# A head's maximum written to the query tile by ScalarE, without a transfer

## The chip, the core and the metric

The kernel runs on one NeuronCore of a Trainium2 chip. The core has five engines that run beside each other and wait for one another by semaphores: TensorE (PE: matmuls, with PEld for its weight loads), VectorE (DVE), ScalarE (ACT), GpSimd (POOL) and SyncE (SP, which issues most DMAs). Sixteen DMA engines move data between HBM and the on-chip memory SBUF; matmul results land in PSUM. The metric is device time in microseconds (us) for one execution: three runs of the kernel before gave a median of 3062.76 us (3058.55 to 3068.89).

## What is computed

Two layers over 2048 tokens of width 1024, batch 1, float32. Layer 0 is a gated linear recurrence beside a pooling mixer. Layer 1, in which the change lies, is forgetting attention with 16 heads of width 64:

```python
q = rms_norm(hd(q), qnorm_g); k = rms_norm(hd(k), knorm_g)      # per head
cumf = jnp.cumsum(log_sigmoid(fl + b_f), axis=1)                # per head, over tokens
logits = q @ k.T * 64 ** -0.5 + cumf[query] - cumf[key]         # masked to key <= query
o = softmax(logits) @ v
o = (o * silu(g)) @ w_out
```

The term cumf[query] is the same for all keys of a query, so the softmax does not depend on it, nor on any other number that is taken from a whole query's logits.

## The kernel before

The tokens are worked in four segments of 512 (`SEG`, s = 0 to 3). For each segment layer 0 runs, then layer 1. In layer 1 a segment's queries attend to the keys of all segments up to their own, so segment s has s old chunks and its own. K, V and bias rows of a segment are stored to DRAM (`k1d`, `k2d`, `vd`) for later segments and loaded again, chunk by chunk, for each head.

All matmuls are in float32r, which rounds; each operand is split in a high and a low part so that the sum keeps float32's accuracy. For a head, `prep` (L1057) makes four tiles of 512 columns: Q1 (high and low part of the queries), Q3 (rows 0 to 63 the high part again, then 4 bias rows), K1 and K2 (rows 0 to 63 the keys' high part, then 4 bias rows). In the product of K2 and Q3 the bias rows add four terms: Q3's first two bias rows are ones against K2's two rows of the negated cumulative log-forget (high and low part); Q3's last two hold minus the query's maximum (high and low part) against K2's rows of ones. The constant rows come from DRAM by two small transfers that ScalarE issues (`q4d`, `cfd`, L1077 and L1078). K2's 68 rows are stored by L1081 and loaded by `old_k2` (L1084) into one of three buffers K2o.

The maximum of each query comes first: `max_pass` (L1089) for head h+1 multiplies Q3 (its maximum rows still 0) with every K2 chunk, 128 queries at a time, and VectorE reduces each product to a column; that runs woven into the attention of head h (`quad_attention`, L1210, and `attend`, L1120), one step of the one after one or two of the other. At its end (L1106 to L1118) VectorE joins the columns to m, a tile of 128 x 4 (query in the partition, block of 128 queries in the column), negates it and splits it in mh and mhl; PE transposes the 8 columns to 8 rows of 128; VectorE copies them to the tile mr; and ScalarE issues a transfer that lays the 8 rows out as the two rows of 512 in Q3. Only then can the first product of K2 and Q3 of that head's attention run.

`attend` walks the chunks: for each old one SyncE loads K1o (two buffers), K2o (three, shared with the max pass) and Vo (two); for each block of 128 keys there are two matmuls into pst, two exponentials on ScalarE (ph and back to pst), the low part pl on VectorE, the row sums la on GpSimd, and two matmuls with the values (pov, pol). Beside that run the projections of the heads to come (`quad_fill`: pqk, pgt, pv), with weights that SyncE loads in four pieces raw of 128 rows each and ScalarE, VectorE and GpSimd split; four tiles of them, sixteen pieces, per four heads. So per head of segment s there are 2s loads K2o, s of K1o, s of Vo and four pieces of weights, and, except in the last segment, one store each of k1d, k2d and vd.

The order of the instructions on each engine is set by a scheduler that places them by priority, which follows the order of the program, as their inputs come ready in its own reckoning; buffers of a pool are taken in the same way. SyncE's queue runs in order: a load that waits for a buffer holds those behind it. The lines that the profile gives for matmuls, transposes and the low parts are those of helpers (L40, L43, L182).

Of the kernel before, what the change touches and what calls it, by code (L numbers as in the profile page):

```python
# [8 lines left out]
F32 = mybir.dt.float32  # L9
F32R = mybir.dt.float32r  # L10
BF16 = mybir.dt.bfloat16
U8 = mybir.dt.uint8
AF = mybir.ActivationFunctionType
ALU = mybir.AluOpType
# [4 lines left out]
P = 128  # L19
T = 2048  # L20
D = 1024
ND = D // P
SEG = 512
NSEG = T // SEG
NTB = SEG // P
NH = 16
HD = 64
VW = 2 * HD + 2
EPS = 1e-6
NEG = -1e30  # L30

# [2 lines left out]
def trunk(ctx, tc, x, cvec, norm_g, ada_c, ada_w, ada_b, ada_bg, lbp, w0, w0o, w1, w1f, w1o,  # L34
          onorm, poolw, pscale, foxb, qkg, out):
    nc = tc.nc
    V, S, G = nc.vector, nc.scalar, nc.gpsimd

    def mm(*a, **k):
        return nc.tensor.matmul(*a, **k)  # L40

    def transpose(o, i):
        return nc.tensor.transpose(o, i, ident[0:i.shape[0], 0:i.shape[0]])  # L43
# [10 lines left out]
    sp = E(tc.tile_pool(name="sp", bufs=2))  # L54
# [8 lines left out]
    def small(shape, name, dt=F32):  # L63
        return sp.tile(shape, dt, name=name, tag=name)
# [22 lines left out]
    def f(ap):  # L87
        return ap.bitcast(F32)
# [32 lines left out]
    for lv in range(NL):  # L121
        half = 1 << lv
        b = 2 * half
# [26 lines left out]

    x1d = dr.tile([T, D], F32, name="x1d")
    k1d = dr.tile([NH, P, T], F32, name="k1d")
    k2d = dr.tile([NH, HD + 4, T], F32, name="k2d")
    vd = dr.tile([NH, P, T // P, VW], F32, name="vd")
    cfd = dr.tile([NH, 4, T], F32, name="cfd")
    q4d = dr.tile([4, SEG], F32, name="q4d")
    gd = dr.tile([2, D], F32, name="gd")


# [816 lines left out]
    def forget_rows(s, act):  # L976
        pf = ps_pj("pfl")

        for d in range(ND):
            for b in range(2):  # L980
                mm(pf[0:48, :], wf[:, d, :], act[:, d, b, :], start=(d + b == 0), stop=(d + b == ND))
        z = tmp("z")[0:NH]
        S.activation(z, pf[0:NH, :], AF.Identity, bias=fb)
        V.tensor_tensor(z, pf[32:32 + NH, :], z, op=ALU.add)
        a = tmp("za")[0:NH]
        S.activation(a, z, AF.Abs)
        S.activation(a, a, AF.Exp, scale=-1.0)
        S.activation(a, a, AF.Ln, bias=1.0)

        V.scalar_tensor_tensor(z, z, 0.0, a, op0=ALU.min, op1=ALU.subtract)  # L990
        cf = tmp("cf")[0:NH]
        V.tensor_tensor_scan(cf, z, zero1[0:NH].to_broadcast([NH, SEG]), fcar, op0=ALU.add, op1=ALU.add)
        V.tensor_copy(fcar, cf[:, SEG - 1:SEG])
        V.tensor_scalar(cf, cf, -1.0, None, op0=ALU.mult)
        ch_ = tmp("cfh", F32R)[0:NH]
        V.tensor_copy(ch_, cf)
        cl = tmp("cfl", F32R)[0:NH]
        split_lo(cl, cf, ch_)
        nc.sync.dma_start(cfd[:, 0, s * SEG:(s + 1) * SEG], f(ch_))
        nc.sync.dma_start(cfd[:, 1, s * SEG:(s + 1) * SEG], f(cl))  # L1000

    seg1 = [dict() for _ in range(NSEG)]

# [53 lines left out]
    def prep(s, h):  # L1057

        L = seg1[s]
        qk = L["qk", h // 2]  # L1060
        j = h % 2
        pt = ps_misc("pqkT")
        for tb in range(NTB):
            transpose(pt[:, tb * P:(tb + 1) * P], qk[:, tb, j * P:(j + 1) * P])
        lo, up = slice(0, HD), slice(HD, P)
        g = col["qkg"]
        Q1 = qp.tile([P, SEG], F32R, name="Q1", tag="qa")
        Q3 = qp.tile([P, SEG], F32R, name="Q3", tag="qb")
        K1 = kp.tile([P, SEG], F32R, name="K1", tag="k1c")
        K2 = kp.tile([P, SEG], F32R, name="K2", tag="k2c")  # L1070
        S.activation(Q1[lo], pt[lo], AF.Copy, scale=g[lo])
        S.activation(K1[up], pt[up], AF.Copy, scale=g[up])
        V.scalar_tensor_tensor(Q1[up], pt[lo], g[lo], f(Q1[lo]), op0=ALU.mult, op1=ALU.subtract)
        V.scalar_tensor_tensor(K1[lo], pt[up], g[up], f(K1[up]), op0=ALU.mult, op1=ALU.subtract)
        S.copy(Q3[lo], f(Q1[lo]))
        S.copy(K2[lo], f(K1[up]))
        nc.scalar.dma_start(f(Q3[HD:HD + 4]), q4d)  # L1077
        nc.scalar.dma_start(f(K2[HD:HD + 4]), cfd[h, :, s * SEG:(s + 1) * SEG])  # L1078
        if s < NSEG - 1:
            nc.sync.dma_start(k1d[h, :, s * SEG:(s + 1) * SEG], f(K1))  # L1080
            nc.sync.dma_start(k2d[h, :, s * SEG:(s + 1) * SEG], f(K2[0:HD + 4]))  # L1081
        L["ops", h] = (Q1, Q3, K1, K2)

    def old_k2(h, c):  # L1084
        K2 = kp.tile([P, SEG], F32R, name="K2o", tag="k2o", bufs=3)
        nc.sync.dma_start(f(K2[0:HD + 4]), k2d[h, :, c * SEG:(c + 1) * SEG])
        return K2

    def max_pass(s, h):  # L1089

        _, Q3, _, K2 = seg1[s]["ops", h]
        mxs = small([P, NTB, NSEG], "mxs")
        for c in range(s + 1):
            kc = K2 if c == s else old_k2(h, c)
            for i in range(NTB):
                n = SEG if c < s else (i + 1) * P
                pm = ps_mx("pmx")
                mm(pm[:, 0:n], Q3[0:HD + 4, i * P:(i + 1) * P], kc[0:HD + 4, 0:n], start=True, stop=True)
                if c < s:
                    V.tensor_reduce(mxs[:, i, c:c + 1], pm[:, 0:n], axis=AX.X, op=ALU.max)  # L1100
                else:
                    V.tensor_tensor_reduce(pm[:, 0:n], pm[:, 0:n], mq[:, SEG - n:], 1.0, NEG, op0=ALU.add,
                                           op1=ALU.max, accum_out=mxs[:, i, c:c + 1])
                if c < s or i < NTB - 1:
                    yield
        m = small([P, NTB], "m")  # L1106
        V.tensor_reduce(m, mxs[:, :, 0:s + 1], axis=AX.X, op=ALU.max)
        mhl = small([P, 2, NTB], "mhl")
        mh = small([P, NTB], "mh", F32R)
        V.tensor_scalar(mh, m, -1.0, None, op0=ALU.mult)  # L1110
        V.tensor_copy(mhl[:, 0, :], f(mh))
        V.scalar_tensor_tensor(mhl[:, 1, :], m, -1.0, f(mh), op0=ALU.mult, op1=ALU.subtract)
        yield
        pt = ps_misc("pmt")
        transpose(pt[0:2 * NTB, 0:P], mhl.rearrange("p a b -> p (a b)"))
        mr = sp.tile([2 * NTB, P], F32R, name="mr", tag="mr", bufs=1)
        V.tensor_copy(mr, pt[0:2 * NTB, 0:P])
        nc.scalar.dma_start(f(Q3[HD + 2:HD + 4].rearrange("a (b t) -> a b t", t=P)), f(mr))  # L1118

    def attend(s, h):  # L1120

# [17 lines left out]
        for c in range(s + 1):  # L1139
            if c < s:  # L1140
                k1 = kp.tile([P, SEG], F32R, name="K1o", tag="k1o", bufs=2)
                nc.sync.dma_start(f(k1), k1d[h, :, c * SEG:(c + 1) * SEG])
                k2 = old_k2(h, c)
                vv = kp.tile([P, NTB, VW], F32R, name="Vo", tag="vo", bufs=2)
                nc.sync.dma_start(f(vv), vd[h, :, c * NTB:(c + 1) * NTB, :])
            else:
                k1, k2, vv = K1, K2, vc[:, :, j, :]
            for b in range(NTB):
                q0 = 0 if c < s else b * P
                ks = slice(b * P, (b + 1) * P)  # L1150
                st = ps_st("pst")
                mm(st[:, q0:], k1[:, ks], Q1[:, q0:], start=True, stop=False)
                mm(st[:, q0:], k2[0:HD + 4, ks], Q3[0:HD + 4, q0:], start=False, stop=(c < s))
                if c == s:
                    mm(st[:, q0:q0 + P], identb, mk, start=False, stop=True)
                ph = tmp("ph", F32R)
                S.activation(ph[:, q0:], st[:, q0:], AF.Exp)  # L1157
                S.activation(st[:, q0:], st[:, q0:], AF.Exp)  # L1158
                pl = tmp("pl", F32R)
                split_lo(pl[:, q0:], st[:, q0:], ph[:, q0:])  # L1160
                if kb == 0:
                    first = f(ph)
                    if s == 0:
                        G.tensor_copy(la, first)
                elif kb == 1 and s > 0:
                    G.tensor_tensor(la, first, f(ph), op=ALU.add)
                else:
                    G.tensor_tensor(la[:, q0:], la[:, q0:], f(ph[:, q0:]), op=ALU.add)  # L1168
                todo.append((b, q0, kb, vv, ph, pl))
                if len(todo) > LAG:  # L1170
                    values(*todo.pop(0))
                kb += 1
                yield
# [108 lines left out]
    def constants():  # L1282
# [15 lines left out]
        V.memset(o1, 1.0)  # L1298
        z1 = tmp("z1")
        V.memset(z1, 0.0)  # L1300
        nc.sync.dma_start(q4d[0:2, :], o1[0:2])
        nc.sync.dma_start(q4d[2:4, :], z1[0:2])
        for s in range(NSEG):
            nc.sync.dma_start(cfd[:, 2, s * SEG:(s + 1) * SEG], o1[0:NH])
            nc.sync.dma_start(cfd[:, 3, s * SEG:(s + 1) * SEG], o1[0:NH])
        wfr = tmp("wfr", F32, (P, ND, NH))
        nc.sync.dma_start(wfr, w1f)
        V.tensor_copy(wf[:, :, 0:NH], wfr)
# [80 lines left out]
```

## Time and profile before

| | us |
|---|---|
| median of three runs | 3062.76 |
| the profiled execution | 3059.16 |
| its span, first to last instruction | 3057.4 |
| PE busy (92%) | 2799.8 |
| DVE busy (78%) | 2373.8 |
| ACT busy (59%) | 1792.8 |
| POOL busy (39%) | 1191.7 |

The span is 1.8 us shorter than the execution. PE is busy most of the time, but its busy time is not all work at full rate, so the time is read from the chain (which step ended last before the next could begin) and from the waits of PE. The granted clock of PE is 0.975 of 2.4 GHz in the mean. 338.56 MB move by DMA, in the mean 111 GB/s.

### The profile page before, as it was taken

To read this page: it belongs to the slowest core of one execution; us is meant where nothing else is said; L and a number is where in the kernel's file an instruction comes from. 1 tells how busy PE (TensorE), PEld (TensorE's weight loads), DVE (VectorE), ACT (ScalarE), POOL (GpSimd) and SP (SyncE) were. 2 spreads that over 40 slices of the span, in tenths; PEclk is the share of its full clock that TensorE was granted. 3 is DMA by queue.
4 is the path that set the end of the run, shared out by engine and by line. 5 is a ranking of instruction groups with operands and counts; after the bars stand their busy time and mean duration, and the time that the engine had idled before them with its cause. 6 is when DMAs were issued, how large, how long until landed. Compare 5 with 4: busy or idle time off the path is not lost.

```text
span 3057.4 us, 49147 instructions
## 1 busy us (share of the span) xinstructions
PE 2799.8 (92%) x17020; PEld 2378.7 (78%) x17020; DVE 2373.8 (78%) x4646; ACT 1792.8 (59%) x3679; POOL 1191.7 (39%) x992
## 2 busy tenths in 40 slices
PE   4999898999998898999999899989999999999998
PEld 4888877879887777779888677777888977676767
DVE  8877688867676888876677888888758688888886
ACT  3454566763545666674445666667544566666674
POOL 3321233323212444434111555554421246655565
PEclk9999999999999999999999999999999999999999
DMA  6423454424234334434234343443333323333342
GB/s 247 163 78 104 120 141 106 122 77 128 73 114 111 101 96 109 130 90 135 68 102 118 111 108 115 117 125 106 115 99 94 110 90 101 103 96 99 92 135 79
DMA packets 198904, 338.56 MB, mean 111 GB/s; under 512 B 19768, under 2 KB 67000, under 8 KB 196096
## 3 DMA queue, kind: packets, MB, share of 16 engines
q1 hardware_dynamic: 195264, 321.52, 36.3%
q10 hardware_dynamic: 3392, 13.90, 1.3%
q8 instruction: 135, 2.21, 0.3%
q14 instruction: 113, 0.93, 0.1%
HBM read 285.72 MB, written 49.36 MB: 110 GB/s over the span
## 4 chain that ended last, share of the span: by engine, by line
PE 49%; DVE 16%; DMA 6%; ACT 5%; issue 3%; POOL 0%; SPq 0%; DVEq 0%; ACTq 0%; POOLq 0%
PE py L40 9%; PE pst L40 6%; PE pgt L40 6%; PE pqk L40 6%; PE pv L40 4%; PE pmx L40 3%; DMA K2o<-k2d 3%; PE pov L40 3%; PE pol L40 2%; PE pq L40 2%; DVE pl L182 2%; PE pl L40 2%; PE pf L40 2%; DVE wt L182 2%; DMA Q<-mr 2%
## 5 line engine op out<-in xcount | busy, mean ns | idle before, releaser
L182 POOL TENSOR_TENSOR wt<-raw,wt 128x512 fp32r<-128x512 f32 x287 | 431.3, 1511 | 998.1 <-ACT wt L293 931.9
L1168 POOL TENSOR_TENSOR la<-la,ph 128x512 f32<-128x512 f32 (+3 forms) x528 | 614.6, 1164 | 445.4 <-ACT ph L1157 396.5
L1157 ACT ACTIVATE ph<-pst 128x512 fp32r<-128x512 f32 (+3 forms) x640 | 341.6, 534 | 277.6 <-PE pst L40 258.6
L182 DVE TENSOR_TENSOR pl<-pst,ph 128x512 fp32r<-128x512 f32 (+3 forms) x640 | 385.7, 604 | 123.2 <-ACT pst L1158 111.1
L40 PE MATMUL pqk<-wt,h 128*128 128x256 f32 x3072 | 457.4, 286 | 5.7 <-DVE h L495 2.6
L40 PEld LDWEIGHTS pqk<-wt,h 128*128 128x128 f32 x3072 | 426.4, 192 | 29.8 <-DVE h L495 3.4
L40 PE MATMUL pgt<-h,wt 128*128 128x512 f32 x1536 | 418.5, 406 | 0.2 <-ACT e L527 0.2
L293 ACT CAST wt<-raw 128x512 fp32r<-128x512 f32 x578 | 337.3, 622 | 72.2 <-PE py L40 33.3
L40 PE MATMUL pv<-wt,h 128*128 128x256 f32 x2304 | 346.9, 295 | 6.0 <-DVE h L182 4.3
L40 PEld LDWEIGHTS pv<-wt,h 128*128 128x128 f32 x2304 | 324.1, 200 | 22.7 <-DVE h L182 6.4
L1158 ACT ACTIVATE pst<-pst 128x512 f32<-128x512 f32 (+3 forms) x640 | 340.1, 531 | 0.0
L40 PEld LDWEIGHTS pgt<-h,wt 128*128 128x128 f32 x1536 | 290.4, 194 | 62.0 <-issue 1.9
L182 DVE TENSOR_TENSOR wt<-raw,wt 128x512 fp32r<-128x512 f32 x291 | 264.2, 912 | 54.7 <-ACT wt L293 53.2
L1100 DVE TENSOR_REDUCE mxs<-pmx 128x1 f32<-128x512 f32 x384 | 258.4, 685 | 46.9 <-PE pmx L40 43.4
L40 PE MATMUL py<-wt,o 128*128 128x256 f32 x1536 | 203.6, 287 | 1.3 <-ACT o L1204 1.2
L40 PE MATMUL py<-wt,mix 128*128 128x256 f32 x1536 | 198.4, 287 | 3.0 <-DVE yt L842 2.1
L40 PEld LDWEIGHTS py<-wt,o 128*128 128x128 f32 x1536 | 194.2, 193 | 7.0 <-ACT o L1204 1.5
L40 PEld LDWEIGHTS py<-wt,mix 128*128 128x128 f32 x1536 | 187.7, 191 | 10.7 <-issue 4.5
L40 PE MATMUL pst<-Q,K2o 68*128 68x512 f32 x384 | 150.2, 412 | 39.6 <-DMA Q<-mr 23.0
L40 PE MATMUL pst<-Q,K1o 128*128 128x512 f32 x384 | 161.9, 427 | 18.8 <-DVE pl L182 18.2
L40 PE MATMUL pov<-ph,Vo 128*128 128x512 f32 x384 | 164.5, 428 | 4.4 <-ACT ph L1157 2.9
L40 PE MATMUL pst<-Q,K 128*128 128x512 f32 (+7 forms) x512 | 131.8, 335 | 37.1 <-DVE pl L182 27.9
(254 smaller groups left out, 5307.4 us busy)
## 6 DMA issues: line engine op xcount, KB each, us to landing
raw<-in_w_dram SPq DMA_DIRECT2D x448, 256.0 KB
K2o<-k2d SPq DMA_DIRECT2D x192, 136.0 KB
Vo<-vd SPq DMA_DIRECT2D x96, 260.0 KB
K1o<-k1d SPq DMA_DIRECT2D x96, 256.0 KB
raw<-in_w1o_dram SPq DMA_DIRECT2D x66, 256.0 KB
raw<-in_w0o_dram SPq DMA_DIRECT2D x64, 256.0 KB
vd<-Vc SPq DMA_DIRECT2D x48, 260.0 KB
ada<-in_ada_w_dram ACTq DMA_DIRECT2D x12, 1024.0 KB
```

The costliest lines, as they stand in the source:

```text
L40: return nc.tensor.matmul(*a, **k)
L182: (eng or V).tensor_tensor(out_t, full, f(hi), op=ALU.subtract)
L293: S.copy(wt[:, 0, sl, :], raw)
L1100: V.tensor_reduce(mxs[:, i, c:c + 1], pm[:, 0:n], axis=AX.X, op=ALU.max)
L1157: S.activation(ph[:, q0:], st[:, q0:], AF.Exp)
L1158: S.activation(st[:, q0:], st[:, q0:], AF.Exp)
L1168: G.tensor_tensor(la[:, q0:], la[:, q0:], f(ph[:, q0:]), op=ALU.add)
```

## The change

Minus the maximum stands in one row of Q3, no longer split in a high and a low part: a rounded number serves as well, since the same one is taken from all logits of a query. With that Q3 and K2 have three bias rows (`KR` = 67 rows in all): row 64 the maximum against ones, rows 65 and 66 ones against the cumulative log-forget. The three DVE operations on m, the tile mr and its transfer are gone. Four transposes of one column of m each write a row of 512 in PSUM, and one ScalarE activation writes it, times -1, to row 64 of Q3. The stores, loads, matmuls and constant rows follow the new row count.

```diff
@@ -26,6 +26,7 @@
 NH = 16
 HD = 64
 VW = 2 * HD + 2
+KR = HD + 3
 EPS = 1e-6
 NEG = -1e30
 
@@ -150,10 +151,10 @@
 
     x1d = dr.tile([T, D], F32, name="x1d")
     k1d = dr.tile([NH, P, T], F32, name="k1d")
-    k2d = dr.tile([NH, HD + 4, T], F32, name="k2d")
+    k2d = dr.tile([NH, KR, T], F32, name="k2d")
     vd = dr.tile([NH, P, T // P, VW], F32, name="vd")
-    cfd = dr.tile([NH, 4, T], F32, name="cfd")
-    q4d = dr.tile([4, SEG], F32, name="q4d")
+    cfd = dr.tile([NH, 3, T], F32, name="cfd")
+    q4d = dr.tile([3, SEG], F32, name="q4d")
     gd = dr.tile([2, D], F32, name="gd")
 
 
@@ -996,8 +997,8 @@
         V.tensor_copy(ch_, cf)
         cl = tmp("cfl", F32R)[0:NH]
         split_lo(cl, cf, ch_)
-        nc.sync.dma_start(cfd[:, 0, s * SEG:(s + 1) * SEG], f(ch_))
-        nc.sync.dma_start(cfd[:, 1, s * SEG:(s + 1) * SEG], f(cl))
+        nc.sync.dma_start(cfd[:, 1, s * SEG:(s + 1) * SEG], f(ch_))
+        nc.sync.dma_start(cfd[:, 2, s * SEG:(s + 1) * SEG], f(cl))
 
     seg1 = [dict() for _ in range(NSEG)]
 
@@ -1074,16 +1075,16 @@
         V.scalar_tensor_tensor(K1[lo], pt[up], g[up], f(K1[up]), op0=ALU.mult, op1=ALU.subtract)
         S.copy(Q3[lo], f(Q1[lo]))
         S.copy(K2[lo], f(K1[up]))
-        nc.scalar.dma_start(f(Q3[HD:HD + 4]), q4d)
-        nc.scalar.dma_start(f(K2[HD:HD + 4]), cfd[h, :, s * SEG:(s + 1) * SEG])
+        nc.scalar.dma_start(f(Q3[HD:KR]), q4d)
+        nc.scalar.dma_start(f(K2[HD:KR]), cfd[h, :, s * SEG:(s + 1) * SEG])
         if s < NSEG - 1:
             nc.sync.dma_start(k1d[h, :, s * SEG:(s + 1) * SEG], f(K1))
-            nc.sync.dma_start(k2d[h, :, s * SEG:(s + 1) * SEG], f(K2[0:HD + 4]))
+            nc.sync.dma_start(k2d[h, :, s * SEG:(s + 1) * SEG], f(K2[0:KR]))
         L["ops", h] = (Q1, Q3, K1, K2)
 
     def old_k2(h, c):
         K2 = kp.tile([P, SEG], F32R, name="K2o", tag="k2o", bufs=3)
-        nc.sync.dma_start(f(K2[0:HD + 4]), k2d[h, :, c * SEG:(c + 1) * SEG])
+        nc.sync.dma_start(f(K2[0:KR]), k2d[h, :, c * SEG:(c + 1) * SEG])
         return K2
 
     def max_pass(s, h):
@@ -1095,7 +1096,7 @@
             for i in range(NTB):
                 n = SEG if c < s else (i + 1) * P
                 pm = ps_mx("pmx")
-                mm(pm[:, 0:n], Q3[0:HD + 4, i * P:(i + 1) * P], kc[0:HD + 4, 0:n], start=True, stop=True)
+                mm(pm[:, 0:n], Q3[0:KR, i * P:(i + 1) * P], kc[0:KR, 0:n], start=True, stop=True)
                 if c < s:
                     V.tensor_reduce(mxs[:, i, c:c + 1], pm[:, 0:n], axis=AX.X, op=ALU.max)
                 else:
@@ -1105,17 +1106,11 @@
                     yield
         m = small([P, NTB], "m")
         V.tensor_reduce(m, mxs[:, :, 0:s + 1], axis=AX.X, op=ALU.max)
-        mhl = small([P, 2, NTB], "mhl")
-        mh = small([P, NTB], "mh", F32R)
-        V.tensor_scalar(mh, m, -1.0, None, op0=ALU.mult)
-        V.tensor_copy(mhl[:, 0, :], f(mh))
-        V.scalar_tensor_tensor(mhl[:, 1, :], m, -1.0, f(mh), op0=ALU.mult, op1=ALU.subtract)
         yield
         pt = ps_misc("pmt")
-        transpose(pt[0:2 * NTB, 0:P], mhl.rearrange("p a b -> p (a b)"))
-        mr = sp.tile([2 * NTB, P], F32R, name="mr", tag="mr", bufs=1)
-        V.tensor_copy(mr, pt[0:2 * NTB, 0:P])
-        nc.scalar.dma_start(f(Q3[HD + 2:HD + 4].rearrange("a (b t) -> a b t", t=P)), f(mr))
+        for i in range(NTB):
+            transpose(pt[0:1, i * P:(i + 1) * P], m[:, i:i + 1])
+        S.activation(Q3[HD:HD + 1], pt[0:1], AF.Copy, scale=-1.0)
 
     def attend(s, h):
 
@@ -1150,7 +1145,7 @@
                 ks = slice(b * P, (b + 1) * P)
                 st = ps_st("pst")
                 mm(st[:, q0:], k1[:, ks], Q1[:, q0:], start=True, stop=False)
-                mm(st[:, q0:], k2[0:HD + 4, ks], Q3[0:HD + 4, q0:], start=False, stop=(c < s))
+                mm(st[:, q0:], k2[0:KR, ks], Q3[0:KR, q0:], start=False, stop=(c < s))
                 if c == s:
                     mm(st[:, q0:q0 + P], identb, mk, start=False, stop=True)
                 ph = tmp("ph", F32R)
@@ -1298,11 +1293,10 @@
         V.memset(o1, 1.0)
         z1 = tmp("z1")
         V.memset(z1, 0.0)
-        nc.sync.dma_start(q4d[0:2, :], o1[0:2])
-        nc.sync.dma_start(q4d[2:4, :], z1[0:2])
+        nc.sync.dma_start(q4d[1:3, :], o1[0:2])
+        nc.sync.dma_start(q4d[0:1, :], z1[0:1])
         for s in range(NSEG):
-            nc.sync.dma_start(cfd[:, 2, s * SEG:(s + 1) * SEG], o1[0:NH])
-            nc.sync.dma_start(cfd[:, 3, s * SEG:(s + 1) * SEG], o1[0:NH])
+            nc.sync.dma_start(cfd[:, 0, s * SEG:(s + 1) * SEG], o1[0:NH])
         wfr = tmp("wfr", F32, (P, ND, NH))
         nc.sync.dma_start(wfr, w1f)
         V.tensor_copy(wf[:, :, 0:NH], wfr)
```

The lines below one another are what PE runs where the attention of head 0 of segment 1 ends and that of head 1 begins (pov and pol are the last value products of the one, pgt is a gate projection, pst with Q and K1o or K2o the first products of the other). Before:

```order
L40 MATMUL pov<-ph,Vc 128x256
L40 MATMUL pol<-pl,Vc 66x256
L43 MATMUL pmt<-ident,mhl 8x128
L40 MATMUL pgt<-h_9623,wt 128x512 x2
L40 MATMUL pov<-ph,Vc 128x128
L40 MATMUL pgt<-h_9623,wt 128x512 x2
L40 MATMUL pol<-pl,Vc 66x128
L40 MATMUL pgt<-h_9623,wt 128x512 x8
L40 MATMUL pst<-Q_10006,K1o 128x512
L40 MATMUL pst<-Q_10007,K2o 128x512
L40 MATMUL pst<-Q_10006,K1o 128x512
```

After:

```order
L41 MATMUL pov<-ph,Vc 128x256
L41 MATMUL pol<-pl,Vc 66x256
L44 MATMUL pmt<-ident,m 1x128 x4
L41 MATMUL pgt<-h_9555,wt 128x512
L41 MATMUL pov<-ph,Vc 128x128
L41 MATMUL pgt<-h_9555,wt 128x512
L41 MATMUL pol<-pl,Vc 66x128
L41 MATMUL pgt<-h_9555,wt 128x512 x10
L41 MATMUL pst<-Q_9938,K1o 128x512
L41 MATMUL pst<-Q_9939,K2o 128x512
L41 MATMUL pst<-Q_9938,K1o 128x512
```

One transpose of 8 columns became four of one column, in the same place: behind the value products of the diagonal's third block and ahead of the next head's first pst. The gate products around it moved by one or two.

SyncE's loads of a head in segment 3 (raw are weights). Before:

```order
L1142 DMA K1o<-k1d 128x512
L1086 DMA K2o<-k2d 68x512
L1145 DMA Vo<-vd 128x520
L1086 DMA K2o<-k2d 68x512
L1142 DMA K1o<-k1d 128x512
L1086 DMA K2o<-k2d 68x512
L288 DMA raw<-in_w_dram 128x512
L1145 DMA Vo<-vd 128x520
L288 DMA raw<-in_w_dram 128x512 x3
```

After:

```order
L1137 DMA K1o<-k1d 128x512
L1087 DMA K2o<-k2d 67x512
L1140 DMA Vo<-vd 128x520
L1087 DMA K2o<-k2d 67x512
L1137 DMA K1o<-k1d 128x512
L1087 DMA K2o<-k2d 67x512
L1140 DMA Vo<-vd 128x520
L289 DMA raw<-in_w_dram 128x512 x4
```

The sequence of the loads is much the same; the loads K2o have 67 rows for 68, and the weights stand together behind the head's last Vo.

## Rows read from the trace of the kernel before

**Rows 1.** The page: busy time and instructions of each engine; the chain's shares by line.
```profile
PE 2799.8 (92%) x17020; PEld 2378.7 (78%) x17020; DVE 2373.8 (78%) x4646; ACT 1792.8 (59%) x3679; POOL 1191.7 (39%) x992
...
PE py L40 9%; PE pst L40 6%; PE pgt L40 6%; PE pqk L40 6%; PE pv L40 4%; PE pmx L40 3%; DMA K2o<-k2d 3%; PE pov L40 3%; PE pol L40 2%; PE pq L40 2%; DVE pl L182 2%; PE pl L40 2%; PE pf L40 2%; DVE wt L182 2%; DMA Q<-mr 2%
```

**Rows 2.** Waits of PE: who waited for what, us in total, times, longest us.
```profile
PE pst L40 <- DMA Q<-mr: 30.9, 14, 6.3
PE pmt L43 <- DVE mhl L1112: 19.0, 20, 1.7
PE pst L40 <- DMA K2o<-k2d: 16.4, 19, 2.0
```

**Rows 3.** Timeline, segment 1's first hand-over: start us, us, engine, line, operation, idle before.
```profile
966.65 0.17 DVE L1110 TENSOR_SCALAR mh<-m 128x4 fp32r<-128x4 f32 x1
...
967.68 0.28 DVE L1117 CAST mr<-pmt 8x128 fp32r<-8x128 f32 x1 [0.60 <-PE pmt L43]
...
967.99 0.65 ACTq L1118 DMA_DIRECT2D Q<-mr  x1
...
976.19 1.22 PE L40 MATMUL pst<-Q,K2o 68*128 68x512 f32 x2 [5.42 <-DMA Q<-mr]
```

**Rows 4.** Instructions on tile u: duration ns min/median/max, first and last start, forms.
```profile
L1179 ACT COPY u<-pov x64: 581/583/585, 376.9 to 3037.5; 64x512 f32<-64x512 f32 x64
```

**Rows 5.** Timeline of PE, a head's end in segment 3.
```profile
2822.07 0.27 PE L43 MATMUL pmt<-ident,mhl 128*8 128x128 f32 x1 [1.15 <-DVE mhl L1112]
2822.18 0.60 PE L43 MATMUL pqkT<-ident,qk 128*128 128x128 f32 x4
```

**Rows 6.** By stretches: engines' busy us (instructions), granted clock, DMA share, GB/s.
```profile
962.30:962.90 0.60, 0.60 (x7) 0.60 (x6) 0.41 (x1) 0.60 (x3) 0.00 (x0) 1.00 0.27 102
2787.00:2787.50 0.50, 0.50 (x3) 0.40 (x3) 0.00 (x0) 0.37 (x1) 0.00 (x0) 0.50 1.05 406
```

**Rows 7.** Timeline of SyncE: a DMA issue of segment 1, then three of segment 3.
```profile
960.72 0.25 SPq L1086 DMA_DIRECT2D K2o<-k2d  x1
...
2777.68 0.28 SPq L1086 DMA_DIRECT2D K2o<-k2d  x1
...
2783.96 1.28 SPq L288 DMA_DIRECT2D raw<-in_w_dram  x3
...
2795.85 0.29 SPq L1086 DMA_DIRECT2D K2o<-k2d  x1
```

**Rows 8.** The chain in order of time: start us, us, what.
```profile
1086.56 2.88 PE pqk L40 x24
...
1185.81 2.87 PE pqk L40 x24
...
1819.49 2.89 PE pqk L40 x24
...
1938.55 2.89 PE pqk L40 x24
...
2761.16 4.66 DMA K2o<-k2d
...
2833.74 3.94 DMA K2o<-k2d
```

**Rows 9.** DMA issues, 2761.1 to 2833.6 us, then 1819.4 to 1938.5 us.
```profile
K2o<-k2d SPq DMA_DIRECT2D x12, 136.0 KB
...
K2o<-k2d SPq DMA_DIRECT2D x16, 136.0 KB
...
k2d<-K SPq DMA_DIRECT2D x4, 136.0 KB
```

**Rows 10.** Timeline of PE, a change of chunk in segment 3.
```profile
2800.44 0.74 PE L40 MATMUL pst<-Q,K2o 68*128 68x512 f32 x2 [0.85 <-DMA K2o<-k2d]
```

**Rows 11.** By stretches around the wait of rows 3.
```profile
966.00:973.00 7.00, 4.77 (x35) 4.27 (x34) 4.22 (x12) 0.59 (x1) 0.00 (x0) 1.00 0.96 150
973.00:979.80 6.80, 3.61 (x13) 3.32 (x14) 2.13 (x6) 2.09 (x4) 1.09 (x1) 0.50 0.60 167
```

## The prediction, made before the changed kernel had run

> **What bounds the kernel now.** I read the page first, then the waits of PE, then the hand-over of one head's maximum in the timeline, then the DMA side by stretches. PE is busy 2799.8 of 3057.4 us and most of the chain; two transfers stand on the chain by name, the load K2o at 3% (some 92 us) and Q<-mr, the one that the change removes, at 2% [rows 1]. Of PE's waits, 30.9 us in 14 waits end with Q<-mr, 19.0 us in 20 with the DVE steps ahead of the transpose, and 16.4 us in 19 with a K2o load [rows 2]. So the transfer that goes is worth at most about 1% of the run, and the transfer that stays, K2o, is already late wherever it is late at all. The profiled execution took 3059.2 us, 3.6 under the median of 3062.8; I sum against it and add the 3.6 at the end.
>
> **What the change removes and adds for the maximum.** Once per head, 64 times, a chain m -> three small DVE operations -> one transpose -> DVE copy -> transfer issued by ScalarE -> first matmul with Q3 becomes m -> four transposes -> one ScalarE activation -> matmul. At the first head hand-over of segment 1 the old chain shows: mh at 966.65, mr copied at 967.68, the issue at 967.99, and the matmul 8.2 us later, after 5.42 us of idle PE [rows 3]. The new activation is 1x512, which no row shows; the nearest is a copy from PSUM of 64x512 at 0.58 us [rows 4]. I take 0.58 and bound it by 0 and 0.8 us. It stands in ScalarE's stream where the DMA issue (0.65 us [rows 3]) stood, and waits for the transposes as the issue waited for the DVE copy, so what is queued behind it there (the copies and exponentials at the head's end) is no later than before. On PE the order keeps the place: transposes, a few products of the next projections, the first matmul with Q3. Three more transposes per head: four in a row take 0.60 us and one takes 0.27 [rows 5], so each further one costs 0.11 us, times 192 is 21 us of PE, at most.
> Term A: of the 30.9 us I take 25 as gone (what is then late is the activation, about 2 us sooner than the transfer); of the 19.0 us I take 8, since m itself is still waited for but the three operations behind it (0.17 us each [rows 3]) are not; 21 are added. Sum -12 us; bounds -50 (all waits gone, the transposes hidden) and +21 (nothing gone).
>
> **What the change does to K2o.** This is the part that decides. K2 keeps one bias row fewer, so each of the 192 loads K2o<-k2d (16 heads x (2 + 4 + 6)) and 48 stores k2d<-K (16 x 3) moves 67 rows of 2 KB and not 68. From 1.6 to 2.2 us after a K2o load's issue at 960.72, with nothing else under way, the DMA share (of all sixteen engines) is 0.27 and the rate 102 GB/s; with three weight loads of 128 rows under way, issued from 2783.96 on, they are 1.05 and 406 GB/s [rows 6, 7]. A quarter: a transfer of 68 rows runs on four of the sixteen engines, one of 128 rows on all. 128 divides by 16; 68 = 4 x 17 divides by 4 and by no larger number up to 16. The plain reading is that the rows are dealt out in equal shares to as many engines as divide them. 67 is a prime: one engine. Of the rows here only this one step is open, since none shows a transfer with a prime number of rows.
> The Trainium skill states such a rule ("DMA: Bandwidth & Descriptors", "Why a DMA increments its semaphore by 16 and not by 1"): a transfer uses the largest number of engines up to 16 that divides the slowest dimension of both sides, and it gives 127 partitions as a case of one engine. By that rule 67 rows go to one engine, the lowest-numbered each time; the shares of a quarter and of all in rows 6 agree with it. With the rule the sum is the one below; without it, that of rival 1.
> The price: one engine moves 406/16 = 25.4 GB/s. 68 rows (139,264 B) at 102 GB/s take 1.37 us, 67 rows (137,216 B) at 25.4 take 5.40 us. Each load lands 4.0 us later, and all of them, the stores too, stand in line on one engine, with that engine's sixteenth of every other transfer behind them (128 rows at 406 GB/s: 0.65 us each).
>
> Term B, segment 3 (attention over three old chunks). Two heads take 2833.74 - 2761.16 = 72.6 us on the chain [rows 8], 36.3 each, with 12 K2o loads in them [rows 9]. Per head the one engine gets 6 x 5.40 = 32.4, and for 3 K1o, 3 Vo and 4 weight loads 10 x 0.65 = 6.5: 38.9 us of work in 36.3. That alone is +2.6 x 16 = +42, the least. But the three K2o buffers let it run ahead only so far: the last load of a head goes out at 2777.68 and the next at 2795.85 [rows 7], and at the change of chunk PE already waits 0.85 us for the load issued 4.6 us earlier [rows 7, 10]. With each load 4.0 us later, each of a head's two chunk changes waits some 4 to 5.4 us more (the load itself, or that and the max pass's load in front of it on the engine). I take +9.4 a head, x16 = +150. At worst nothing overlaps the stretch without loads, some 15 us (18 less the landing of the last load): 38.9 + 15 - 36.3 = +17.6 a head, +280.
> Term C, segment 2. Four heads take 1938.55 - 1819.49 = 119.1 us [rows 8], 29.8 each; 16 loads and 4 stores in them [rows 9]. Per head 5 x 5.40 = 27.0, and for 2 K1o, 2 Vo, 4 weights, the k1d and vd stores 10 x 0.65 = 6.5: 33.5 in 29.8, at least +3.7 x 16 = +60. With one chunk change and a store that a load can meet I take +8, x16 = +128; at worst +18.7 (the same 15 us uncovered), +300.
> Term D, segment 1. 1185.81 - 1086.56 = 99.2 us for four heads, 24.8 each; 3 x 5.40 + 8 x 0.65 = 21.4 fits. I take +1.5, x16 = +24; 0 to +64 (one load uncovered per head).
> Term E, weights whose sixteenth waits behind one or two K2o on that engine, and the first max pass of each segment, which no attention covers: +20, 0 to +60.
> Term F, the clock. After the 5.42 us wait of rows 3 the granted clock was 0.50 for a stretch of 6.8 us, 1.00 ahead of it [rows 11]: 1.2 for 2.4 GHz. I expect some 56 new waits of this size in segments 2 and 3; with one in four followed by such a stretch at up to 3.4 us each, +48, less what the next load hides anyway: +40, 0 to +190.
> All the rest (three bias rows from q4d and cfd in place of four, one constant store fewer per segment, 67 for 68 rows in the matmuls, whose columns stay) I set at 0: those transfers are 6 to 8 KB and issued a head ahead.
> Sum: -12 + 150 + 128 + 24 + 20 + 40 = +350. 3059.2 + 350 + 3.6 = 3413, said as 3410 us.
>
> **Rivals.**
> 1. The 67 rows keep four engines, or more: the share of a quarter then comes from something other than divisibility. Then only A is left, 3059.2 - 12 + 3.6 = 3051 us, faster. For it: the two shares of rows 6 are just two points. Against: if rows were spread as evenly as they go, 68 would have used more than four engines. It decides from the point where a 67-row load lands as soon as a 68-row one. Chance 0.07, of which 0.05 faster and 0.02 within the 0.3% that a measurement here can tell from no change.
> 2. One engine, but the loads run ahead well enough that only its total work counts: 3059.2 - 12 + 42 + 60 + 3.6 = 3153, slower. For it: three buffers, and a stretch of 18 us per head without a load. Against: PE already waits at the chunk changes. Chance 0.13.
> 3. One engine, and nothing covers: the loads in line, then the diagonal part of the head. Terms at their upper ends for B and C, middle for the rest: 3059.2 - 12 + 280 + 300 + 24 + 20 + 40 + 3.6 = 3715. For it: SyncE issues in order, so a load that waits for a buffer holds the K1o, Vo and weights behind it. Against: two of the three buffers come free before the diagonal part, so the next head's first loads can run beside it. Chance 0.15.
> My forecast has 0.65, with 3260 to 3570 as its own range. The range over all reaches halfway to rivals 2 and 3: 3190 to 3640. Faster 0.05, same 0.02, slower 0.93.
>
> **What would show it.** Right: in a stretch where only a K2o load moves, a DMA share of 0.06 to 0.07 and 25 GB/s; PE's waits for K2o up from 16.4 us to some hundreds, the most in segments 2 and 3; K2o far above 3% of the chain; segment 3's heads at about 45 us, segment 2's at 38, layer 0 unchanged. For term A: no wait for Q<-mr, a wait for the activation of a few us in all. Wrong: heads of 36 us in segment 3, or a K2o load at a share of a quarter; then rival 1 holds and the kernel is a little faster.

## The result and the profile after

The changed kernel takes 3385.1 us (median of 4 runs, 3379.6 to 3387.9), the kernel before 3064.7 in the same comparison (4 runs, 3058.6 to 3068.9): 1.1045 times as long, with a 95% interval of 1.1021 to 1.107. The forecast was 3410 us. The profiled execution took 3384.5 us with a span of 3382.7, at a mean granted clock of 0.927 (0.975 before).

The page: busy time and instructions of each engine, and the chain's shares by line (the lines of [rows 1]).

```profile
PE 2928.3 (87%) x17212; PEld 2475.6 (73%) x17212; DVE 2330.1 (69%) x4390; ACT 1828.6 (54%) x3743; POOL 1167.3 (35%) x992
...
DMA K2o<-k2d 13%; PE py L41 9%; PE pgt L41 8%; PE pst L41 6%; PE pqk L41 6%; PE pv L41 4%; PE pmx L41 4%; PE pov L41 3%; PE pf L41 2%; PE pq L41 2%; PE pol L41 2%; PE pl L41 2%; DVE wt L183 1%; ACT wt L294 1%; ACT ph L1152 1%
```

K2o stands at the head of the chain with 13%, where it had 3%, and Q<-mr is gone from it. PE is busy 128.5 us longer, of which 192 more transposes at 0.11 us would make 21: the matmuls themselves have become slower, which the clock of 0.927 already hints at. The waits of PE (who waited for what, us in total, times, longest us; beside [rows 2]):

```profile
PE pst L41 <- DMA K2o<-k2d: 187.9, 41, 12.4
...
PE pmx L41 <- DMA K2o<-k2d: 30.1, 8, 7.9
...
PE pmx L41 <- DMA Q<-q4d: 7.1, 8, 1.4
```

218.0 us in 49 waits end with a K2o load, against 16.8 in 20 before (the 16.4 in 19 of [rows 2], and one of 0.4 at pmx). No wait for Q<-mr is left; the wait that could have taken its place, for the activation, is 2.3 us in 4.

What one load now is, in two stretches in which nothing else is transferred (start and end, length, busy us and instructions of PE, PEld, DVE, ACT and POOL, granted clock, DMA share, GB/s; beside [rows 6]):

```profile
1795.00:1799.00 4.00, 0.00 (x0) 0.00 (x0) 0.00 (x0) 0.00 (x0) 0.00 (x0) 0.55 0.07 26
2976.00:2981.00 5.00, 3.12 (x8) 2.15 (x8) 1.38 (x2) 0.00 (x0) 0.00 (x0) 0.54 0.07 26
```

The share is 0.07 of sixteen, one engine (1/16 = 0.0625), at 26 GB/s; with 68 rows it was 0.27 and 102. In the first stretch no engine computes anything: the whole core stands still for one transfer. A second load had been issued by then (the last line below), and the share is still that of one engine: the two stand in line on the same one. Why that one is so late shows in SyncE's timeline ahead of it (segment 2: start, us, queue, line, what it issues):

```profile
1785.53 0.24 SPq L1082 DMA_DIRECT2D k2d<-K  x1
...
1788.73 0.32 SPq L1137 DMA_DIRECT2D K1o<-k1d  x1
1789.15 0.27 SPq L1087 DMA_DIRECT2D K2o<-k2d  x1
...
1791.45 0.52 SPq L1087 DMA_DIRECT2D K2o<-k2d  x1
```

The store k2d, 67 rows too, went out 3.6 us before the load. At 5.4 us each the two take 10.8 one after the other; from the issue of the store at 1785.53 to the end of the load on the chain at 1800.05 it is 14.5, with the start of the first and a sixteenth of K1o and the weights between them. The chain has the load at 10.90 us, in the first of these pieces (start us, us, what):

```profile
1789.15 10.90 DMA K2o<-k2d
...
1941.39 11.38 DMA K2o<-k2d
...
2910.40 9.09 DMA K2o<-k2d
...
2923.13 7.77 DMA K2o<-k2d
...
3007.24 9.03 DMA K2o<-k2d
```

They also give the length of a head, each mark standing at the same place of the order: four heads of segment 2 take 1941.39 - 1789.15 = 152.2 us, 38.1 each (29.8 before), and two of segment 3 take 3007.24 - 2910.40 = 96.8, 48.4 each (36.3 before, [rows 8]).

The new instructions of the maximum (operation, count, ns min/median/max, first and last start, forms):

```profile
L44 PE MATMUL pmt<-ident,m x256: 270/272/421, 357.8 to 3333.6; 128*1 128x128 f32 x128
L1113 ACT ACTIVATE Q<-pmt x64: 585/586/590, 358.5 to 3333.9; 1x512 fp32r<-1x512 f32 x64
```

The activation on one partition takes 586 ns, as the copy on 64 partitions did (583 ns, [rows 4]).

What a long wait does to TensorE, in its timeline in segment 3 (start, us, engine, line, operation, count, idle time before and what ended it):

```profile
2877.16 0.40 PE L41 MATMUL pov<-ph,Vo 128*128 128x512 f32 x1
2881.17 0.77 PE L41 MATMUL pmx<-K2o,Q 67*128 67x512 f32 x1 [3.60 <-DMA K2o<-k2d]
...
2882.58 0.63 PE L41 MATMUL pmx<-K2o,Q 67*128 67x512 f32 x1
```

A matmul of 512 columns takes 0.40 us ahead of the wait and 0.63 behind it, and starts follow each other at some 0.43 us instead of 0.24. The granted clock of the 6 us behind the wait is 0.50, the lower of the two levels (1.2 for 2.4 GHz):

```profile
2881.20:2887.20 6.00, 6.00 (x14) 4.62 (x15) 1.97 (x3) 0.91 (x2) 0.17 (x1) 0.50 0.09 32
```

### The profile page after: what moved, and what is told of

It is laid out like the page before. It is cut to its first block, busy times and chain, and to the rows that moved or that the text cites. A ratio compares the mean times of both kernels' runs of the same rounds, so it can differ in the third digit from the quotient of the medians.

```text
span 3382.7 us, 49256 instructions
## 1 busy us (share of the span) xinstructions
PE 2928.3 (87%) x17212; PEld 2475.6 (73%) x17212; DVE 2330.1 (69%) x4390; ACT 1828.6 (54%) x3743; POOL 1167.3 (35%) x992
## 4 chain that ended last, share of the span: by engine, by line
PE 54%; DMA 17%; DVE 15%; ACT 10%; issue 4%; POOL 1%; SPq 0%; ACTq 0%; DVEq 0%; POOLq 0%
DMA K2o<-k2d 13%; PE py L41 9%; PE pgt L41 8%; PE pst L41 6%; PE pqk L41 6%; PE pv L41 4%; PE pmx L41 4%; PE pov L41 3%; PE pf L41 2%; PE pq L41 2%; PE pol L41 2%; PE pl L41 2%; DVE wt L183 1%; ACT wt L294 1%; ACT ph L1152 1%
## 5 line engine op out<-in xcount | busy, mean ns | idle before, releaser
L1163 POOL TENSOR_TENSOR la<-la,ph 128x512 f32<-128x512 f32 (+3 forms) x528 | 602.4, 1141 | 843.8 <-ACT ph L1152 816.3
L183 POOL TENSOR_TENSOR wt<-raw,wt 128x512 fp32r<-128x512 f32 x287 | 419.1, 1468 | 1012.8 <-ACT wt L294 962.2
L41 PE MATMUL pgt<-h,wt 128*128 128x512 f32 x1536 | 434.9, 421 | 0.1
L41 PE MATMUL pv<-wt,h 128*128 128x256 f32 x2304 | 354.9, 299 | 3.7 <-DVE h L183 3.2
L41 PEld LDWEIGHTS pgt<-h,wt 128*128 128x128 f32 x1536 | 306.4, 204 | 69.1 <-issue 2.1
L41 PEld LDWEIGHTS pv<-wt,h 128*128 128x128 f32 x2304 | 333.9, 205 | 24.8 <-DVE h L183 5.2
L41 PE MATMUL pst<-Q,K2o 67*128 67x512 f32 x384 | 179.4, 476 | 196.5 <-DMA K2o<-k2d 187.9
L41 PEld LDWEIGHTS pst<-Q,K2o 67*128 67x128 f32 x384 | 83.4, 222 | 226.6 <-DMA K2o<-k2d 210.1
L41 PE MATMUL pmx<-K2o,Q 67*128 67x512 f32 x384 | 182.1, 482 | 49.3 <-DMA K2o<-k2d 30.1
L41 PE MATMUL pst<-Q,K1o 128*128 128x512 f32 x384 | 170.9, 446 | 32.2 <-DVE pl L183 32.0
```

What stands on the lines that cost most here:

```text
L183: (eng or V).tensor_tensor(out_t, full, f(hi), op=ALU.subtract)
```

## The experiments

Ratios are to the kernel before in the same comparison, with 95% intervals; its median was 3064.7, 3051.3, 3040.9 and 3044.8 us in the four comparisons, so ratios are compared, not medians. My theory: the row count of the K2 transfers is the whole loss, by the one engine and by loads that start too late to be hidden. The rivals: the new maximum chain costs something itself; or it is the engine's total work, and not the lateness of each load.

**The change, with 68 rows in the K2 transfers again** (a fourth bias row of ones rides along, used by nothing).

```diff
+KS = HD + 4
-    k2d = dr.tile([NH, KR, T], F32, name="k2d")
+    k2d = dr.tile([NH, KS, T], F32, name="k2d")
...
-            nc.sync.dma_start(k2d[h, :, s * SEG:(s + 1) * SEG], f(K2[0:KR]))
+            nc.sync.dma_start(k2d[h, :, s * SEG:(s + 1) * SEG], f(K2[0:KS]))
...
-        nc.sync.dma_start(f(K2[0:KR]), k2d[h, :, c * SEG:(c + 1) * SEG])
+        nc.sync.dma_start(f(K2[0:KS]), k2d[h, :, c * SEG:(c + 1) * SEG])
```

> The changed kernel, but K2 stored and loaded with 68 rows (a fourth bias row of ones that no matmul reads); matmuls, transposes and the ScalarE write as changed. Theory (67 rows run on one DMA engine, and that is the whole loss): a load is back at a DMA share of 0.25, PE's waits for K2o near 16 us, and the time is that of before less term A, about 3050 us (3035 to 3068). Rival (the new chain of the maximum, its four transposes, or the moved order carry part of the loss): 3100 us or more.

Measured: 3033.1 us, ratio 0.9946 (0.993 to 0.9963), 2 us under the theory's range, which was reckoned from a kernel before of 3062.8 us where this comparison's took 3051.3. One row more in the transfer gives back the whole loss and leaves the gain of the maximum chain alone: about 16 us (11 to 21). A lone load has its quarter of the engines back, and PE's waits for K2o are 24.3 us, nearer to the 16.8 of the kernel before than to 218.0, if not quite the 16 said. From the stretches and the waits of this kernel:

```profile
1029.40:1030.20 0.80, 0.80 (x6) 0.54 (x5) 0.80 (x4) 0.36 (x2) 0.59 (x1) 1.00 0.26 102
```

```profile
PE pst L42 <- DMA K2o<-k2d: 24.3, 17, 5.4
```

This kernel does the same work as the changed one, matmul for matmul, so the two show stage by stage what the loss consists of. Layer 1 of segments 1, 2 and 3, the changed kernel first, then this one (columns as in the stretches above):

```profile
898.70:1463.20 564.50, 515.24 (x3234) 441.11 (x3235) 420.02 (x777) 350.05 (x741) 211.49 (x178) 0.96 0.36 106
1613.40:2378.60 765.20, 624.67 (x3554) 521.46 (x3555) 496.38 (x905) 419.24 (x869) 293.24 (x242) 0.89 0.32 95
2530.30:3366.60 836.30, 678.56 (x3484) 546.67 (x3485) 530.12 (x932) 440.65 (x899) 359.41 (x290) 0.88 0.25 78
```

```profile
890.10:1431.40 541.30, 504.30 (x3234) 432.75 (x3235) 418.03 (x777) 349.73 (x741) 213.32 (x178) 0.98 0.39 111
1583.00:2226.50 643.50, 593.65 (x3554) 498.76 (x3555) 497.90 (x905) 417.43 (x869) 294.12 (x242) 0.97 0.38 114
2375.00:3016.10 641.10, 605.99 (x3484) 492.88 (x3485) 525.37 (x932) 439.74 (x899) 361.00 (x290) 0.99 0.32 103
```

Segment 1 loses 23.2 us, segment 2 121.7, segment 3 195.2: 340 of the 350.3 us between the two spans. (By the ratios the loss is 0.1099 of 3064.7, 337 us: the kernels before of the two comparisons lie 13 us apart, so a stage's figure is good to a few us.) For the same 3554 and 3484 matmuls PE is busy 31.0 and 72.6 us longer, and the granted clock falls from 0.97 and 0.99 to 0.89 and 0.88. The rest is idle time. PE's waits for K2o in segments 2 and 3, the changed kernel first:

```profile
PE pst L41 <- DMA K2o<-k2d: 87.9, 12, 12.4
...
PE pmx L41 <- DMA K2o<-k2d: 7.9, 1, 7.9
...
PE pst L41 <- DMA K2o<-k2d: 99.2, 28, 5.4
PE pmx L41 <- DMA K2o<-k2d: 22.2, 7, 3.7
```

```profile
PE pst L42 <- DMA K2o<-k2d: 17.7, 7, 5.4
...
PE pst L42 <- DMA K2o<-k2d: 6.6, 10, 2.2
```

They grow by 78.1 and 114.8 us. So of the 316.9 us of the two stages 192.9 are waits and 103.6 are slower matmuls, which leaves 20 for everything else. In segment 1 it is not the waits for K2o (0.9 us). PE is busy 10.9 us longer and waits longer for ScalarE's ph; in the changed kernel:

```profile
PE pov L41 <- ACT ph L1152: 11.1, 9, 3.4
...
PE pst L41 <- DMA K2o<-k2d: 0.9, 1, 0.9
```

With 68 rows:

```profile
PE pov L42 <- ACT ph L1153: 1.4, 6, 0.3
```

**The kernel before, with 67 rows in the K2 transfers** (and in the matmuls that read K2), and nothing else of the change.

```diff
-        nc.sync.dma_start(f(K2[0:HD + 4]), k2d[h, :, c * SEG:(c + 1) * SEG])
+        nc.sync.dma_start(f(K2[0:KR]), k2d[h, :, c * SEG:(c + 1) * SEG])
...
-                mm(st[:, q0:], k2[0:HD + 4, ks], Q3[0:HD + 4, q0:], start=False, stop=(c < s))
+                mm(st[:, q0:], k2[0:KR, ks], Q3[0:KR, q0:], start=False, stop=(c < s))
```

> The kernel before, with its transfer Q<-mr, its split maximum and one transpose, but K2 stored, loaded and multiplied with 67 rows (the low part of the maximum is laid out and not used). Theory (the row count alone makes the loss): 3385 us plus what the new chain of the maximum gave, 3385 to 3430 us, K2o loads on one engine at 25 GB/s. Rival (the order of the changed kernel or its new chain is needed for the loss): below 3300 us.

Measured: 3436.9 us, ratio 1.1263 (1.1237 to 1.1289), 7 us over the theory's range. The row count alone makes the loss, and more of it than the whole change, whose 1.1045 lies 2.2% below. The waits of PE show why:

```profile
PE pst L41 <- DMA K2o<-k2d: 157.3, 43, 8.0
PE pst L41 <- DMA Q<-mr: 106.8, 47, 6.8
```

Q<-mr, 30.9 us in the kernel before, is at 106.8: a transfer of 4 KB issued by another engine is late as well when the K2o loads fill one DMA engine. It is the transfer that is slow, not only what goes before it: from its issue to the end of the last of its eight packets pass 4.3 us in the median of segments 1 to 3, where it is 1.4 us in the kernel before. To have it gone is worth some 67 us here (2.2% of 3051), where it is worth 16 beside short loads.

**The change, with 80 rows** (13 rows of zeros ride along: 80 = 16 x 5).

```diff
+KS = HD + 16
-    cfd = dr.tile([NH, 3, T], F32, name="cfd")
+    cfd = dr.tile([NH, 16, T], F32, name="cfd")
+            nc.sync.dma_start(cfd[:, 3:16, s * SEG:(s + 1) * SEG], z1[0:NH].unsqueeze(1).to_broadcast([NH, 13, SEG]))
```

> The changed kernel with K2 padded to 80 rows in its transfers (13 rows of zeros that no matmul reads), which 16 divides. Theory (as many engines as divide the rows): sixteen engines, a load in some 0.4 us of transfer, PE's waits for K2o under 10 us, 3040 us (3015 to 3060), a little faster than with 68 rows. Rival (a share fixed at four engines for tiles under 128 rows): as with 68 rows, a load at a share of 0.25 for 1.6 us. If bytes and not engines counted, 80 rows would be slower than 67.

Measured: 3056.6 us, ratio 1.0019 (1.0005 to 1.0034). That is in the range, but the gain over 68 rows did not come, and the waits for K2o are not under 10 us. The profile, which is of the fastest of eight executions (3043.5 to 3059.3 us), names one place:

```profile
PE pd L42 <- DVE kT L535: 24.3, 1, 24.3
...
PE pst L42 <- DMA K2o<-k2d: 15.6, 8, 5.4
```

The waits for K2o fall from 24.3 us to 15.6, so the longer transfer is no later than the one of 68 rows. The shortest load that ran alone took 0.84 us from its first packet to its last, 0.4 said. But PE waits 24.3 us once, near the start, a wait that the kernel with 68 rows does not have: SyncE writes the zeros among the constants, and the weights behind them go out at 89.0 us and not at 53.3. So the miss is put down to this edit's own start-up; no run moved the zeros elsewhere, and the profile does not show the 13 us by which the median lies above it.

**The change, with K2 moved as 64 rows and its three bias rows apart.**

```diff
-        nc.sync.dma_start(f(K2[0:KR]), k2d[h, :, c * SEG:(c + 1) * SEG])
+        nc.sync.dma_start(f(K2[0:HD]), k2d[h, :, c * SEG:(c + 1) * SEG])
+        nc.sync.dma_start(f(K2[HD:KR]), cfd[h, :, c * SEG:(c + 1) * SEG])
```

> The changed kernel with K2 stored and loaded as 64 rows, and the three bias rows loaded by a second transfer of 3 rows straight from cfd (192 more transfers that SyncE issues). Theory: 64 rows run on sixteen engines, 3 rows on three, both short; PE's waits for K2o under 15 us; 3045 us (3015 to 3070), the second transfer costing SyncE some 0.3 us each, off the path. Rival (each more transfer on the path costs its own latency of some 2 to 3 us where a chunk changes): 3080 us or more.

Measured: 3012.9 us, ratio 0.9879 (0.9864 to 0.9895), better than the theory's range and faster than both kernels in spite of 192 more issues. The waits for the two transfers together are 9.8 us:

```profile
PE pst L41 <- DMA K2o<-k2d: 5.2, 3, 3.2
PE pst L41 <- DMA K2o<-cfd: 4.6, 1, 4.6
```

**The same split in the kernel before** (64 rows and four bias rows), to see what is left of the new maximum chain.

```diff
-        nc.sync.dma_start(f(K2[0:HD + 4]), k2d[h, :, c * SEG:(c + 1) * SEG])
+        nc.sync.dma_start(f(K2[0:HD]), k2d[h, :, c * SEG:(c + 1) * SEG])
+        nc.sync.dma_start(f(K2[HD:HD + 4]), cfd[h, :, c * SEG:(c + 1) * SEG])
```

> The kernel before, transfer Q<-mr and all, with K2 stored and loaded as 64 rows and its four bias rows loaded by a second transfer from cfd. It shows what the change to the maximum is worth where no load is late: against the changed kernel with the same split (3013 us). Theory (term A is worth some 16 us and does not hang on the loads): 3025 to 3040 us. Rival (the split alone makes the gain and the new chain of the maximum nothing): 3008 to 3018 us.

Measured: 3020.9 us, ratio 0.9936 (0.9915 to 0.9958). In us that lies between the two ranges, which were set beside 3013 us from a comparison whose kernel before was 10 us slower; the ratios decide. Against the split with the change, 0.9879, the new chain is worth 0.57%, as in the first experiment (0.54%): the two gains add up.

**A fourth K2o buffer.** If the engine's total work were the bound, starting loads earlier would give little back. The buffer needs room, so both kernels of the pair have one work tile fewer.

```diff
-    tp = E(tc.tile_pool(name="tp", bufs=9))
+    tp = E(tc.tile_pool(name="tp", bufs=8))
-        K2 = kp.tile([P, SEG], F32R, name="K2o", tag="k2o", bufs=3)
+        K2 = kp.tile([P, SEG], F32R, name="K2o", tag="k2o", bufs=4)
```

The first edit alone, the control:

> The changed kernel with eight scratch buffers of the tmp tag in place of nine: the control for the next run, which needs their memory. Every theory: 3385 to 3430 us, since the waits for K2o stay as they are.

Both edits:

> The same with four buffers K2o in place of three. Theory of the prediction (in segments 2 and 3 the loads cannot be issued early enough, because their three buffers come free late; the one engine's total work is below the time): the waits for K2o shrink and the time falls by 60 us or more against the control, towards the 3153 us at which only the engine's total work counts. Rival (the one engine is full, so issuing earlier only makes the line longer): within 25 us of the control, with the engine busy in nearly all of segments 2 and 3.

Measured: 3372.2 us for the control, ratio 1.1089 (1.1052 to 1.1127), no less than the change's own 1.1045, and 3241.7 with the fourth buffer, 1.066 (1.0631 to 1.0689). The buffer gives back 130.5 us with no byte less on the engine. The waits for K2o, the control first:

```profile
PE pst L41 <- DMA K2o<-k2d: 189.0, 41, 12.3
...
PE pmx L41 <- DMA K2o<-k2d: 31.9, 10, 7.8
```

```profile
PE pst L41 <- DMA K2o<-k2d: 79.6, 32, 5.1
```

With 5.4 us at pmx the waits for K2o are 85.0 us, where they were 220.9; PE's waits for ScalarE's ph rise from 34.2 to 60.2 us. So the larger part of the waits was lateness: with three buffers a load is issued too late to be hidden.

**The change, with 74 rows** (seven rows of zeros, written by VectorE; 74 = 2 x 37), a count between the two.

```diff
+KS = HD + 10
+        V.memset(f(K2[HD:KS]), 0.0)
-        nc.sync.dma_start(f(K2[0:KR]), k2d[h, :, c * SEG:(c + 1) * SEG])
+        nc.sync.dma_start(f(K2[0:KS]), k2d[h, :, c * SEG:(c + 1) * SEG])
```

> The changed kernel with 74 rows in K2's transfers (VectorE writes zeros to ten rows before the bias rows land; no matmul reads the seven more). 74 is 2 x 37. Theory (as many engines as divide the rows): two engines, 37 rows of 80 ns each, 2.96 us of transfer between the 1.4 us of 68 rows and the 5.4 us of 67; a DMA share of 0.13 and 51 GB/s; time 3060 to 3160 us, nearer to 68 rows than to 67 since most of the 1.6 us more per load find cover. Rival (bytes or a fixed number of engines for all tiles under 128 rows): 3035 to 3050 us as with 68 rows.

Measured: 3137.1 us, ratio 1.0315 (1.0294 to 1.0336). A lone load shows two engines:

```profile
990.00:991.60 1.60, 1.60 (x13) 1.20 (x11) 1.38 (x3) 1.28 (x3) 1.13 (x2) 1.00 0.13 51
```

Shares of 0.07, 0.13 and 0.26 for 67, 74 and 68 rows are one, two and four sixteenths. 74 rows are more bytes than 68 and 67, and lie between them in time; no rule by bytes gives that order.

Where no share can be read, because a load is too short, the packets tell the engines. A load that runs alone shows one packet per row and beside them as many packets under 512 B as it has engines by its share. In order, 67 rows (the changed kernel, 2875 to 2881 us), 68 (2052.4 to 2054.3), 74 (2704.5 to 2708), 80 (2799.7 to 2800.7), and 64 with the three bias rows apart (2777.1 to 2778.2):

```profile
DMA packets 68, 0.14 MB, mean 23 GB/s; under 512 B 1, under 2 KB 1, under 8 KB 68
...
DMA packets 72, 0.14 MB, mean 73 GB/s; under 512 B 4, under 2 KB 4, under 8 KB 72
...
DMA packets 76, 0.15 MB, mean 43 GB/s; under 512 B 2, under 2 KB 2, under 8 KB 76
...
DMA packets 96, 0.16 MB, mean 164 GB/s; under 512 B 16, under 2 KB 16, under 8 KB 96
...
DMA packets 86, 0.14 MB, mean 125 GB/s; under 512 B 19, under 2 KB 19, under 8 KB 86
```

By this count 80 rows run on sixteen engines, and the 19 of the split are sixteen for 64 rows and three for 3. A rule by factors of two alone would have given the 3 rows one.

**68 rows stored, 67 loaded**: the first experiment's kernel with the load alone cut.

```diff
-        nc.sync.dma_start(f(K2[0:KS]), k2d[h, :, c * SEG:(c + 1) * SEG])
+        nc.sync.dma_start(f(K2[0:KR]), k2d[h, 0:KR, c * SEG:(c + 1) * SEG])
```

> The changed kernel with K2 stored with 68 rows (four engines) and loaded with 67 (one engine): the 192 loads alone on the slow shape, the 48 stores not. Theory (the wait for a load at a change of chunk is the loss; nothing waits for a store, which only stands in line with the loads in segments 1 and 2): 3330 to 3380 us, segment 3, which stores nothing, unchanged at 836 us, segment 2 shorter by some 10 to 50 us. Rival (stores carry half or more of segments 1 and 2's loss): segment 2 down by 60 us or more, in all below 3320 us.

Measured: 3302.8 us, ratio 1.0849 (1.0833 to 1.0866), below the theory's range and within what the rival gave for the whole. The 192 loads carry most of the loss, 1.0849 - 0.9946 = 9.0% of the time before; with the 48 stores at 68 rows the other 2.0 of the 11.0 are gone, more than was expected of them. Stage by stage, by the marks of the chain, segment 2, where a load meets a store on the engine, is 38 us shorter than in the changed kernel (727.0 for 765.2), as the theory had it, and segment 1 is 17 shorter, most of the 23 that it had lost. Segment 3 is 18 us shorter too (818.6 for 836.3, and 837.0 in the control with eight work tiles), although it stores nothing; its waits for K2o are 110.5 us for 121.4. That was not expected, and no run settles it, so not all of the 2.0 is shown to be the stores'.

**The split, with the fourth buffer**: is anything left to gain?

```diff
-    tp = E(tc.tile_pool(name="tp", bufs=9))
+    tp = E(tc.tile_pool(name="tp", bufs=8))
-        K2 = kp.tile([P, SEG], F32R, name="K2o", tag="k2o", bufs=3)
+        K2 = kp.tile([P, SEG], F32R, name="K2o", tag="k2o", bufs=4)
```

> The changed kernel with 64 rows and three bias rows as two transfers, and four buffers K2o and eight tmp in place of three and nine. Theory (with sixteen engines the loads are no longer late, 10 us of waits in all are left, so a fourth buffer has nothing to give): 3005 to 3020 us, as the split alone at 3013. Rival (SyncE's queue still holds weights and K1o behind a load that waits for a buffer): 2985 to 3003 us.

Measured: 3008.8 us, ratio 0.9875 (0.9854 to 0.9896), the split's own 0.9879 within the interval. Where the loads are short, an earlier start buys nothing.

## Why the prediction was right

**One engine for 67 rows**, the step that was open, holds: share 0.07, 26 GB/s, and 0.13 at 74 rows. The Trainium skill's rule ("DMA: Bandwidth & Descriptors", "Why a DMA increments its semaphore by 16 and not by 1") gives one, two and four engines for 67, 74 and 68 rows, and these shares agree with it. Rival 1, four engines or more and 3051 us, falls with the rows of the 67-row load and with 3385 us.

**The sum.** Measured against the 68-row kernel, which has the new maximum chain already:

| term | predicted | measured |
|---|---|---|
| A, the maximum chain | -12 | -16 (-21 to -11) |
| B and C, segments 3 and 2, with F, the clock | +150 +128 +40 = +318 | +195.2 +121.7 = +317 |
| D, segment 1 | +24 | +23 |
| E, and the rest outside these stages | +20 | +10 |

The measured column adds up to +334; kernel against kernel the change is +320 (3385.1 less 3064.7), the rest being the 13 us between the two comparisons. So the +350 was some 30 us high.

The parts inside the second row were not right. The waits grew by 114.8 us in segment 3 and 78.1 in segment 2 where B and C said 150 and 128; slower matmuls took 103.6 us where F said 40. Per head the waits grew by 7.2 and 4.9 us, where B and C had set 9.4 and 8. They are 48 in the two segments where 17 had been, 31 more and not 56: 35 of 3.5 us in segment 3, and in segment 2 just 13, of 7.4 us.

What failed for F is the assumption that one wait in four is followed by a stretch at half clock. The trace's records of the granted clock have 53 stretches at 0.50 in the two segments, 375 us together, beside the 48 waits; in the 68-row kernel they have 17, 61 us together, beside its 17: about one a wait. Each of the 36 more costs 2.9 us (103.6/36). F's 3.4 us was itself read too high: the low stretch of [rows 11] begins at 973.0, inside the wait that ends at 976.19 [rows 3], and PE is busy in 3.61 of its 6.8 us, so that one cost at most 1.8. The two errors, 85 and 64 us, cancel to a large part, and the 20 us that neither holds close the sum; that it fits to 1 us is luck, its size is not.

D's figure is luck too. It stood for some 1.5 us of uncovered load in each head, and segment 1 waits 0.9 us for K2o in all; the 23 us are a busier PE and a later ScalarE, and 17 of them go with the short stores. Why ScalarE is later there is not shown. E's 10 us are what the stages leave over; no run measures E's own waits. The lower end of the range, 3190, is a little below halfway from the forecast's own range to rival 2 (3206), which changes nothing here.

**The heads** came out at 48.4 us in segment 3 (45 said) and 38.1 in segment 2 (38), and layer 0 as it was: from the end of a segment's layer 1 to the end of the next one's layer 0 pass 150.2 and 151.7 us on the chain, 153.2 twice before.

**Rival 2**, only the engine's total work counts (3153 us), falls with the time, and the fourth buffer shows why: 130.5 us come back although the work on the engine is the same. What remains at 1.066 is still more than that rival's 1.03 (3153/3062.8), so even four buffers don't make it the only bound. **Rival 3**, nothing covers (3715 us), was not reached: 48.4 us a head in segment 3, its case was 53.9.

**The maximum chain** did what it says. No transfer is waited for, the activation takes 586 ns for 580 said, and its waits are 2.3 us. It brings 0.5%, twice measured.

## What to carry to other kernels

Before the number of rows in a transfer is changed, if only by one, read from a lone transfer's DMA share how many engines it runs on, and factor the new number: here one bias row saved cost 11%, one useless row gives it back, and 64 rows with the odd three apart beat both kernels. Price a slower transfer where it is waited for, from the issue that its buffer allows and with the stores that share its engine; then add the clock, since here slower matmuls behind the waits cost half as much time as the waits themselves. A gain that is real (0.5% for the maximum chain) must be timed apart from what rides along with it.

## What the runs showed that was not expected

- With 48 waits of some 4.5 us in segments 2 and 3 the granted clock of whole stages fell from 0.97 and 0.99 to 0.89 and 0.88, for 104 us of slower matmuls. This is read from profiles; no run kept the waits and changed the clock alone.
- One filled DMA engine delays transfers of other queues and other sizes: Q<-mr from 30.9 to 106.8 us of waits in the kernel before with 67 rows, and perhaps the three rows of Q<-q4d, for which PE waits 7.1 us in the changed kernel and not at all with 68 rows.
- The part ahead of layer 1 of segment 1, which loads old K2 just three times, is 9 us longer than with 68 rows (898.7 for 890.1 us to its end). With 68 rows stored and 67 loaded, that part is no longer than with all at 68 (885.9 us), so the stores are suspected; no run tells how they do it.
- The time follows the engines of a K2 load: ratios of 1.1045, 1.0315 and 0.9946 for one, two and four, and 0.9879 for 64 rows on sixteen with the bias rows apart. The 80 rows, on sixteen too, stand at 1.0019 with their start-up.
